# First loads in another order, tables through Pool's queue, and D0's probabilities in a zero-padded field of 384 queries

## The chip, the cores and the metric

One core of a Trainium2 chip runs the whole program. The metric is the device time of one execution in microseconds; the kernel before takes 1674.26 us (median of three runs, 1674.24 to 1674.72). Engines: TensorE (PE; its weight loads are PEld), VectorE (DVE), ScalarE (ACT), GpSimd (POOL) and SyncE (SP), which here only issues DMAs. DMAs issued by SP go through queue q1, those issued by Pool through q0.

## The reference

Two layers of an encoder on 512 tokens of 1024 features. In each layer the normed input is projected to queries, keys and values of four attention branches, to gates and to merge weights. A is a banded attention (128 either way) with 8 query heads on 2 key heads, a learned bias by distance and a sink; B a difference of two dense attentions with bias; C a dense one with rotated queries and keys; D three groups of 8 heads with strides 1, 4 and 16, each in a band of 64 either way (in its own stride) with bias, joined by their softmax sums.

```python
for l in range(DEPTH):
    h = _rmsnorm(x, norm_gain[l])
    p = _project(h, w_in[l])
    ...  # oa, ob, oc, od from p; biases from rel_bias by bucketed distance
    for n, o in enumerate((oa, ob, oc, od)):
        gated = o * jax.nn.silu(p['gate'][..., n * BRANCH_W:(n + 1) * BRANCH_W])
        y = gated @ w_branch[l, n]
        merged = merged + jax.nn.sigmoid(p['merge'][..., n * D_MODEL:(n + 1) * D_MODEL]) * y
    x = x + merged @ w_out[l]
```

Group D0 (stride 1) is what the second half of the change is about: query i sees keys i - 64 to i + 64.

## The kernel before

**Split numbers.** Matmuls run in fp16 on pairs (high part, low part). A weight piece of 1 MB comes as two fp32 halves (`wst`, `dma_w`, L118), which `load_w` (L129) splits: ScalarE makes `whi` (L142), VectorE `wlo` (L143). Activations lie transposed in `hT_h` and `hT_l`. One projection is three matmuls per 128 features (L396 to L398 for token-major results, L407 to L409 for feature-major ones), so a token tile of 512 columns takes 24.

**Start.** SP loads x tile 0, the norm gain, weight piece 0, x tile 1, piece 1, x tile 2, a small table `rb`, the one-hot table `oh` (97 rows of 4,864 bytes), x tile 3, and then weights. `wst` has three buffers, so the fourth half waits until VectorE is done with the first. `norm_a` (L209) norms a token tile; `norm_b` (L229) transposes it on TensorE into PSUM (L253) and splits it from there; `norm_t` (L239) splits first and transposes by DMA. Tiles 0 to 2 take `norm_b`, tile 3 takes `norm_t`.

**Bias lines.** The biases depend on distance alone. `bias_lines` (L260) multiplies `oh` by the table of 36 heads' biases (L274), six products with results on 8 partitions (one a head), copied into `acc`. One DMA (L929) then writes `lines` in DRAM: 23 copies of 8 rows of 2,432 numbers (9,728 bytes), 1.79 MB. `load_bias` (L536) reads a bias tile from the copies, so that each partition gets its shift. In the code the products stand behind the first token tile of the A queries, the write behind A's keys and values.

**Small tables.** Pool loads gain tables, the rotation table and the setup tables (`gain_tables`, `setup_columns`, `setup`) through its own queue at the start of the program; VectorE works them up.

**Order.** The Tile framework orders each engine's instructions by a simulated timeline; `tc.issue_after(x)` keeps what stands under it behind instruction x. `weave` interleaves the steps of an attention with those of projections. Every engine runs in order.

**D0.** `attn_d0` (L797). For a head, scores are taken for four blocks of 128 keys (kb), each against the queries from 64 ahead of the block to 64 behind it, a field of 256 columns (192 for the first and last block). ScalarE and VectorE turn them into probabilities `ph` (high) and `pl` (low). The value products for a block of 128 queries (qb) take the probabilities as the stationary operand. From the block's own keys all 128 queries count; from the block ahead only the first 64, from the one behind only the last 64. So `lo` and `hi`, 64 partitions each, are products of their own, and the first and last query blocks have their own block cut in two as well. A head has ten products of 64 queries and two of 128, each of three matmuls (`pv_mm`, L563). A's values (L658) have ten products of 128 queries a head.

Of the kernel before, what the change touches and what calls it, by code (L numbers as in the profile page):

```python
# [85 lines left out]
)  # L86
PIECE = 128 * 2048
AHEAD = 3


@with_exitstack
def encoder(ctx, tc, x, wf, norm_gain, qk_gain, sink, lambda_vec, sub_gain, rel_bias, onehot, rope, out):
# [83 lines left out]
    def load_x(src, tt):  # L176
        if tt % 2 == 0:
            x_sb[tt // 2] = qk.tile([128, 2, D], F32, tag="qx", name="xt", bufs=2)
        nc.sync.dma_start(out=x_sb[tt // 2][:, tt % 2, :], in_=src[tt * 128:tt * 128 + 128, :])

    gain_b = {}

# [19 lines left out]
    load_x(x, 1)  # L202
    with tc.issue_after(dma_w(1).ins):
        load_x(x, 2)
        nc.sync.dma_start(out=rb, in_=bass.AP(tensor=rel_bias.tensor, offset=rel_bias.offset, ap=[[0, 3], [36, 32], [1, 36]]))
        nc.sync.dma_start(out=oh, in_=onehot)
        load_x(x, 3)

    def norm_a(l, tt):  # L209

        xt = x_sb[tt // 2][:, tt % 2, :]
        ss = sm.tile([128, 2], F32, tag="n_ss", name="ss")
        for j in range(2):
# [6 lines left out]
        S.activation(rs, ln, AF.Exp, scale=-0.5)  # L220
        hs = []
        for j in range(2):
            f = slice(512 * j, 512 * j + 512)
            h = tmp.tile([128, 512], F32, tag="gs", name="h", bufs=4)
            V.scalar_tensor_tensor(h, xt[:, f], rs, gain_b[l][:, f], op0=ALUm, op1=ALUm)
            hs.append(h)
        return hs

    def norm_b(tt, hs):  # L229

        for j in range(2):
            tr = transpose4(hs[j])
            d = slice(4 * j, 4 * j + 4)
            c = slice(tt * 128, tt * 128 + 128)
            S.activation(hT_h[:, d, c], tr, AF.Copy, scale=SH)
            done = V.scalar_tensor_tensor(hT_l[:, d, c], tr, SH, hT_h[:, d, c], op0=ALUm, op1=ALUs)
        return done

    def norm_t(tt, hs):  # L239

        hi = tmp.tile([128, 2, 512], F16, tag="st", name="h_hi", bufs=3)
        lo = tmp.tile([128, 2, 512], F16, tag="st", name="h_lo", bufs=3)
# [17 lines left out]
    def bias_lines():  # L260

        V.tensor_scalar(rb, rb, SB, None, op0=ALUm)
        V.tensor_copy(rb16[0:96, :], rb)
        for a in (32, 64):
            r = slice(a, a + 32)
            V.tensor_tensor(rb[r, :], rb[r, :], rb16[r, :], op=ALUs)
            V.tensor_copy(rb16[r, :], rb[r, :])
        V.tensor_tensor(rb16[64:96, :], rb[64:96, :], rb16[64:96, :], op=ALUs)
        for i, (s0, ln_, h0, nh, off, w) in enumerate(SEG.values()):
            for e in range(0, ln_, 512):  # L270
                n = min(512, (ln_ + 1 - e))
                c = slice(s0 + e, s0 + e + n)
                p = ps_mm.tile([128, 512], F32, tag="mm", name="p")
                PE.matmul(p[:8, :n], rb16[:, h0:h0 + 8], oh[:, c], start=True, stop=True)  # L274
                if i % 2:
                    S.activation(accf[0:8, c], p[:8, :n], AF.Copy, scale=1.0 / SB)
                else:
                    V.tensor_scalar(accf[0:8, c], p[:8, :n], 1.0 / SB, None, op0=ALUm)
# [165 lines left out]
    def proj_q(res, l, kind, col, perm=False):  # L444
# [4 lines left out]
        for tt in range(NT):  # L449
# [9 lines left out]
            st = tmp.tile([128, 4, 4, HD], F16, tag="st", name="st", bufs=3)  # L459
# [10 lines left out]
    def proj_k(res, l, kind, col, perm=False):  # L470
# [6 lines left out]
        for tt in range(NT):  # L477
# [4 lines left out]
            st = tmp.tile([128, 16, 128], F16, tag="st", name="st", bufs=3)  # L482
            hi = st[:, 0:8, 0:HD]
            S.activation(hi, heads(kg), AF.Copy, scale=KS)
            V.scalar_tensor_tensor(st[:, 8:16, 0:HD], heads(kg), KS, hi, op0=ALUm, op1=ALUs)
            V.tensor_copy(st[:, :, HD:128], st[:, :, 0:HD])
            nc.sync.dma_start_transpose(out=kk[:, :, tt * 128:tt * 128 + 128], in_=st.rearrange("p a d -> p (a d)"))
            yield

    VS = SV / PROJ  # L490
# [20 lines left out]
    def proj_kv(res, l, kind, col):  # L511
# [6 lines left out]
        for tt in range(NT):  # L518
# [7 lines left out]
            st = tmp.tile([128, 4, 128], F16, tag="st", name="st", bufs=3)  # L526
# [59 lines left out]
    def gated(n, ft, gd):  # L586

        if ft == 0:
            gT[n] = big.tile([128, 4, 2, T], F16, tag="gT", name="gT", bufs=2)
        st = tmp.tile([128, 2, 512], F16, tag="st", name="st", bufs=3)  # L590
# [206 lines left out]
    def attn_d0(l, qs, kk, rsk, v):  # L797
        bias, o, n12 = {}, {}, {}

        def scores(h):  # L800
            if h % 4 == 0:
                bias[h // 4] = load_bias("D0", h, 4, "bias_d0")
            ph, pl = new_p()
            for kb in range(4):
                q0, q1 = max(128 * kb - 64, 0), min(128 * kb + 192, T)
                n, f0 = q1 - q0, q0 - (128 * kb - 64)
# [2 lines left out]
                s_mm(p, kk[:, h, ks], kk[:, 8 + h, ks], qs[:, h, q0:q1])  # L809
                t = at.tile([128, 512], F32, tag="t", name="t", bufs=3)[:, :n]  # L810
                V.scalar_tensor_tensor(t, p, rsk[:, kb, h:h + 1], bias[h // 4][:, h % 4, f0:f0 + n], op0=ALUm, op1=ALUa)  # L811
                f = slice(f0, f0 + n)
                probs(t, n, nm[:, l, 12 + h:13 + h], ph[:, kb, f], pl[:, kb, f])
            return ph, pl

        def values(h, pp):
# [6 lines left out]
                                  in_=dsc[2][hp].rearrange("(t p) e -> p t e", p=128))  # L823
            pv = ps_pv.tile([128, 4, 66], F32, tag="pv", name="pv")
            for qb in range(4):
                vt = [v[:, k, h] for k in range(4)]
                lo, hi = pv[0:64, qb, 0:65], pv[64:128, qb, 0:65]
                if qb > 0:
                    k = qb - 1
                    pv_mm(lo, ph[:, k, 192:256], pl[:, k, 192:256], vt[k], HD, True, False)  # L830
                if qb < 3:
                    k = qb + 1
                    pv_mm(hi, ph[:, k, 0:64], pl[:, k, 0:64], vt[k], HD, True, False)
                if qb == 0:
                    pv_mm(lo, ph[:, 0, 64:128], pl[:, 0, 64:128], vt[0], HD, True, True)
                    pv_mm(hi, ph[:, 0, 128:192], pl[:, 0, 128:192], vt[0], HD, False, True)
                elif qb == 3:
                    pv_mm(lo, ph[:, 3, 64:128], pl[:, 3, 64:128], vt[3], HD, False, True)
                    pv_mm(hi, ph[:, 3, 128:192], pl[:, 3, 128:192], vt[3], HD, True, True)
                else:  # L840
                    pv_mm(pv[:, qb, 0:65], ph[:, qb, 64:192], pl[:, qb, 64:192], vt[qb], HD, False, True)
# [73 lines left out]
    for l in range(L):  # L915
# [5 lines left out]
        if l:  # L921
            norm_t(3, last)
        else:
            bias_lines()
            with tc.issue_after(normed.ins):
                gain_tables(0)
        run(qa, proj_kv(r, l, "A", 512))
        if l == 0:
            nc.sync.dma_start(out=lines.rearrange("c h n -> h c n"),  # L929
                              in_=accf[0:8, 0:LINE].unsqueeze(1).to_broadcast([8, COPIES, LINE]))  # L930
            with tc.issue_after(normed.ins):
                setup_columns()
                setup()
        weave(attn_a(l, r["qA"], *r["kA"], r["vA"]),
# [90 lines left out]
```

## Time and profile before

| | |
|---|---|
| median of the runs | 1674.26 us |
| the profiled execution | 1674.46 us |
| its span (first to last instruction) | 1672.4 us |
| TensorE busy | 1602.6 us (96%) |
| VectorE busy | 1075.9 us (64%) |
| ScalarE busy | 961.0 us (57%) |
| Pool busy | 8.8 us (1%) |
| mean granted TensorE clock | 0.985 |

Busy time is the union of an engine's instructions. TensorE's matmuls overlap in the pipeline, so its pace is read from their starts. In the slices a digit is the busy share of a fortieth of the span in tenths; PEclk is the clock granted to TensorE, where 0.5 stands for its level of 1.2 GHz and 1.0 for 2.4. In a timeline row stand start, duration, engine, line and operation, out<-in, count, and in brackets the idle time ahead and what ended it.

### The profile page before, as it was taken

How to read it: one execution, taken by the hardware profiler on the slowest of the kernel's cores; microseconds unless marked ns; L12 is line 12 of the kernel's file. 1: busy time of each engine (PE TensorE's matmuls, PEld its weight loads, DVE VectorE, ACT ScalarE, POOL GpSimd, SP SyncE). 2: the span in 40 equal slices, each digit the busy share in tenths (PEclk: the TensorE clock that was granted, in tenths of full speed). 3: DMA queues.
4: the chain of work that ended last, by engine and by line, in shares of the span. 5: the costliest groups of instructions: out<-in, count | busy, mean ns of one | idle time of the engine just before them, and what ended most of it. 6: DMA issues, size and time to landing. Idle time of an engine off the chain costs nothing.

```text
span 1672.4 us, 26438 instructions
## 1 busy us (share of the span) xinstructions
PE 1602.6 (96%) x10302; PEld 834.6 (50%) x10302; DVE 1075.9 (64%) x2104; ACT 961.0 (57%) x1771; POOL 8.8 (1%) x32
## 2 busy tenths in 40 slices
PE   3389999999999999999999999999999999999999
PEld 1155545564555554454445554556455555445444
DVE  3368866785576766575556887678457676657451
ACT  3157676566664656564545767556667464556450
POOL 1000000000000000000000000000000000000000
PEclk8699999999999999999999999999999999999999
DMA  5974733352356757435357483336235674753421
GB/s 188 97 161 133 164 109 95 100 133 76 110 121 155 183 144 191 141 114 143 109 169 173 105 183 119 93 101 133 76 98 130 152 180 132 200 146 94 133 88 51
DMA packets 230817, 218.37 MB, mean 131 GB/s; under 512 B 176316, under 2 KB 188620, under 8 KB 230509
## 3 DMA queue, kind: packets, MB, share of 16 engines
q1 hardware_dynamic: 229925, 214.26, 50.0%
q0 software_dynamic: 768, 2.43, 0.5%
q8 instruction: 80, 1.31, 0.3%
q14 instruction: 44, 0.36, 0.1%
HBM read 163.94 MB, written 10.24 MB: 104 GB/s over the span
## 4 chain that ended last, share of the span: by engine, by line
PE 89%; DMA 6%; DVE 3%; ACT 1%; issue 0%; SPq 0%; DVEq 0%; ACTq 0%
PE mm L396 15%; PE mm L397 15%; PE mm L398 15%; PE mm L407 10%; PE mm L409 10%; PE mm L408 10%; PE s L560 3%; PE s L561 3%; PE pv L565 3%; DMA hT_h<-h_hi 2%; PE pv L567 2%; PE pv L566 2%; DMA oh<-in_onehot_dram 1%; DMA wst<-in_wf_dram 1%; DMA qs<-st 1%; DVE wlo L143 1%
## 5 line engine op out<-in xcount | busy, mean ns | idle before, releaser
L396 PE MATMUL mm<-whi,hT_h 128*128 128x512 f16 (+1 forms) x1408 | 522.7, 371 | 38.7 <-DMA hT_h<-h_hi 31.1
L397 PE MATMUL mm<-wlo,hT_h 128*128 128x512 f16 (+1 forms) x1408 | 522.6, 371 | 0.7 <-DVE wlo L143 0.7
L398 PE MATMUL mm<-whi,hT_l 128*128 128x512 f16 (+1 forms) x1408 | 522.2, 371 | 1.2 <-DMA hT_l<-h_lo 1.2
L143 DVE SCALAR_TENSOR_TENSOR wlo<-wst,whi 128x1024 f16<-128x1024 f32 (+1 forms) x260 | 307.3, 1204 | 203.1 <-ACT whi L142 202.0
L142 ACT ACTIVATE whi<-wst 128x1024 f16<-128x1024 f32 (+1 forms) x260 | 262.6, 1036 | 269.4 <-PE mm L408 122.3
L396 PEld LDWEIGHTS <-hT_h 128*128 128x128 f16 x1408 | 144.4, 103 | 175.9 <-DMA hT_h<-h_hi 32.1
L398 PEld LDWEIGHTS <-hT_l 128*128 128x128 f16 x1408 | 144.4, 103 | 147.6 <-issue 2.6
L397 PEld LDWEIGHTS <-hT_h 128*128 128x128 f16 x1408 | 144.4, 103 | 146.4 <-issue 7.7
L407 PE MATMUL mm<-hT_h,whi 128*128 128x512 f16 x512 | 194.1, 379 | 0.0
L409 PE MATMUL mm<-hT_h,wlo 128*128 128x512 f16 x512 | 194.1, 379 | 0.0
L408 PE MATMUL mm<-hT_l,whi 128*128 128x512 f16 x512 | 194.0, 379 | 0.0
L551 ACT ACTIVATE t<-t,nm 128x512 f32<-128x512 f32 (+2 forms) x224 | 132.0, 599 | 69.1 <-DVE t L811 24.1
L556 DVE TENSOR_TENSOR pl<-t,ph 128x512 f16<-128x512 f32 (+2 forms) x224 | 119.1, 543 | 37.8 <-ACT ph L555 36.5
L565 PE MATMUL pv<-v,ph 128*128 128x65 f16 (+2 forms) x992 | 123.8, 202 | 0.1
L566 PE MATMUL pv<-v,ph 128*128 128x64 f16 (+2 forms) x992 | 122.9, 201 | 0.0
L567 PE MATMUL pv<-v,pl 128*128 128x65 f16 (+2 forms) x992 | 121.0, 199 | 0.0
L409 PEld LDWEIGHTS <-wlo 128*128 128x128 f16 x768 | 75.1, 98 | 88.9
L407 PEld LDWEIGHTS <-whi 128*128 128x128 f16 x768 | 75.1, 98 | 87.1
L408 PEld LDWEIGHTS <-whi 128*128 128x128 f16 x768 | 75.1, 98 | 86.6
L555 ACT ACTIVATE ph<-t 128x512 f16<-128x512 f32 (+2 forms) x224 | 110.9, 506 | 2.8 <-PE pv L567 0.7
L560 PE MATMUL s<-qs,kk 128*128 128x512 f16 (+4 forms) x384 | 99.4, 293 | 1.7 <-DVE gs L582 1.3
L561 PE MATMUL s<-qs,kk 128*128 128x512 f16 (+4 forms) x384 | 100.5, 292 | 0.0
(173 smaller groups left out, 1925.4 us busy)
## 6 DMA issues: line engine op xcount, KB each, us to landing
wst<-in_wf_dram SPq DMA_DIRECT2D x264, 512.0 KB
dsc<-num SPq DMA_DIRECT2D x16, 260.0 KB
xt<-in_x_dram SPq DMA_DIRECT2D x8, 512.0 KB
bias_b<-lines SPq DMA_DIRECT2D x8, 448.0 KB
bias_a<-lines SPq DMA_DIRECT2D x16, 192.0 KB
num<-dsc SPq DMA_DIRECT2D x8, 260.0 KB
n<-dsc SPq DMA_DIRECT2D x8, 260.0 KB
bias_d<-lines SPq DMA_DIRECT2D x32, 64.0 KB
```

Of the source, the lines that this page charges most:

```text
L142: S.activation(hi[:, a], st[:, e:e + step], AF.Copy if sc is SW else AF.Identity, scale=sc)
L143: V.scalar_tensor_tensor(lo[:, a], st[:, e:e + step], sc, hi[:, a], op0=ALUm, op1=ALUs)
L396: PE.matmul(p[:, :ncol], a, wh, start=(k == 0), stop=False)
L397: PE.matmul(p[:, :ncol], a, wl, start=False, stop=False)
L398: PE.matmul(p[:, :ncol], b, wh, start=False, stop=(k == 7))
L407: PE.matmul(p, wh[:, k, f], rh[:, k], start=(k == 0), stop=False)
L408: PE.matmul(p, wh[:, k, f], rl[:, k], start=False, stop=False)
L409: PE.matmul(p, wl[:, k, f], rh[:, k], start=False, stop=(k == nk - 1))
L561: PE.matmul(p, klo, q, start=False, stop=True)
L565: PE.matmul(o, ph, vt[:, 0:d + 1], start=start, stop=False)
L566: PE.matmul(o[:, 0:d], ph, vt[:, d + 2:2 * d + 2], start=False, stop=False)
L567: PE.matmul(o, pl, vt[:, 0:d + 1], start=False, stop=stop)
```

## The change

SP loads x, gain and the first two weight pieces, and then only weights. `wst` has five buffers. `rb` and `oh` go to Pool's queue, where all tables stand behind a copy of one element of the last x tile (`there`). All four token tiles of the first layer go through `norm_b`. The products of the bias lines stand behind A's keys and values. Their stationary operand `rbr` now holds 16 copies of a segment's 8 heads (five copies on VectorE), so results lie on 128 partitions, and two DMAs on Pool's queue write `lines` from 128 and from 56 partitions. Keys (16 blocks of 128) are split and transposed in two halves. In D0 the field is 384 columns wide, the outer 64 on both sides set to zero by Pool, and each value product takes 128 columns.

```diff
+WST = 5
-            st = wp.tile([128, 1024], F32, tag="wst", name="wst", bufs=3)
+            st = wp.tile([128, 1024], F32, tag="wst", name="wst", bufs=WST)
...
         load_x(x, 2)
-        nc.sync.dma_start(out=rb, in_=bass.AP(tensor=rel_bias.tensor, offset=rel_bias.offset, ap=[[0, 3], [36, 32], [1, 36]]))
-        nc.sync.dma_start(out=oh, in_=onehot)
-        load_x(x, 3)
+        last_x = load_x(x, 3)
+
+    there = const.tile([128, 1], F32, name="there")
+    tables = G.tensor_copy(there, x_sb[1][:, 1, 0:1])
...
+        rbr = const.tile([97, len(SEG), 128], F16, name="rbr")
         for i, (s0, ln_, h0, nh, off, w) in enumerate(SEG.values()):
+            V.tensor_copy(rbr[:, i].rearrange("p (c h) -> p c h", h=8),
+                          rb16[:, h0:h0 + 8].unsqueeze(1).to_broadcast([97, 16, 8]))
...
-                PE.matmul(p[:8, :n], rb16[:, h0:h0 + 8], oh[:, c], start=True, stop=True)
+                PE.matmul(p[:, :n], rbr[:, i], oh[:, c], start=True, stop=True)
...
+        for c0, c1_ in ((0, 16), (16, COPIES)):
+            nc.gpsimd.dma_start(out=lines[c0:c1_].rearrange("c h n -> (c h) n"), in_=accf[0:8 * (c1_ - c0), 0:LINE])
 
     for tt in range(NT):
-        normed = (norm_b if tt < 3 else norm_t)(tt, norm_a(0, tt))
-        if tt < 2:
-            load_w(tt)
+        normed, split = norm_b(tt, norm_a(0, tt))
+        if tt == 0:
+            with tc.issue_after(scaled[0].ins):
+                load_w(0)
+            with tc.issue_after(split.ins):
+                load_w(1)
...
+            for pp in (ph, pl):
+                G.memset(pp[:, :, 0:64], 0.0)
+                G.memset(pp[:, :, 320:384], 0.0)
...
-                f = slice(f0, f0 + n)
+                f = slice(f0 + 64, f0 + 64 + n)
...
-                vt = [v[:, k, h] for k in range(4)]
-                lo, hi = pv[0:64, qb, 0:65], pv[64:128, qb, 0:65]
...
+                kbs = [k for k in (qb - 1, qb, qb + 1) if 0 <= k < 4]
+                for kb in kbs:
+                    f = slice((qb - kb + 1) * 128, (qb - kb + 2) * 128)
+                    pv_mm(pv[:, qb, 0:65], ph[:, kb, f], pl[:, kb, f], v[:, kb, h], HD, kb == kbs[0], kb == kbs[-1])
...
-            bias_lines()
-            with tc.issue_after(normed.ins):
+            with tc.issue_after(normed.ins), tc.issue_after(tables.ins):
                 gain_tables(0)
+                nc.gpsimd.dma_start(out=rb, in_=bass.AP(tensor=rel_bias.tensor, offset=rel_bias.offset,
+                                                        ap=[[0, 3], [36, 32], [1, 36]]))
+                nc.gpsimd.dma_start(out=oh, in_=onehot)
         run(qa, proj_kv(r, l, "A", 512))
         if l == 0:
-            nc.sync.dma_start(out=lines.rearrange("c h n -> h c n"),
-                              in_=accf[0:8, 0:LINE].unsqueeze(1).to_broadcast([8, COPIES, LINE]))
+            bias_lines()
```

SP's queue at the start of the program, before (`xt` are x tiles, `hT_h` the transposed activations):

```order
L179 DMA xt<-in_x_dram 128x1024
L186 DMA gain_b<-in_norm_gain_dram 128x1024
L125 DMA wst<-in_wf_dram 128x1024 x2
L179 DMA xt<-in_x_dram 128x1024
L125 DMA wst<-in_wf_dram 128x1024 x2
L179 DMA xt<-in_x_dram 128x1024
L205 DMA rb<-in_rel_bias_dram 96x1x36
L206 DMA oh<-in_onehot_dram 97x2432
L179 DMA xt<-in_x_dram 128x1024
L125 DMA wst<-in_wf_dram 128x1024 x3
L929 DMA lines<-acc 8x23x2432
```

The same queue after the change:

```order
L180 DMA xt<-in_x_dram 128x1024
L187 DMA gain_b<-in_norm_gain_dram 128x1024
L126 DMA wst<-in_wf_dram 128x1024 x2
L180 DMA xt<-in_x_dram 128x1024
L126 DMA wst<-in_wf_dram 128x1024 x2
L180 DMA xt<-in_x_dram 128x1024 x2
L126 DMA wst<-in_wf_dram 128x1024 x9
L478 DMA_TRANSPOSE qs<-st 128x8x128 x2
```

The tables and `lines` have left it, the last x tile stands ahead of all weights but the first two pieces, and nine weight halves stand ahead of the first query transposes.

TensorE behind A's keys and values, after the change (L281 the products of the bias lines, L575 and L576 the scores of A's first head, L409 to L411 gate 0):

```order
L281 MATMUL p<-oh,rbr 128x512
L575 LDWEIGHTS kk
L575 MATMUL s<-qs,kk 128x384
L576 LDWEIGHTS kk
L576 MATMUL s<-qs,kk 128x384
L281 LDWEIGHTS rbr
L281 MATMUL p<-oh,rbr 128x384
L281 LDWEIGHTS rbr
L281 MATMUL p<-oh,rbr 128x256
L281 LDWEIGHTS rbr
L281 MATMUL p<-oh,rbr 128x256
L409 LDWEIGHTS hT_h
```

Before, the same six products (L274) stood between the second and the third token tile's transposes. Now they stand between the first three scores, and 52 products of gate 0 follow ahead of the next score.

TensorE at a head of D0, before (the first of its 12 products; the shape's first number is the queries):

```order
L409 MATMUL mm<-gT,wlo 128x512
L565 LDWEIGHTS ph
L565 MATMUL pv<-v,ph 64x65
L566 LDWEIGHTS ph
L566 MATMUL pv<-v,ph 64x64
L567 LDWEIGHTS pl
L567 MATMUL pv<-v,pl 64x65
```

and after:

```order
L422 MATMUL mm<-gT,wlo 128x512
L580 LDWEIGHTS ph
L580 MATMUL pv<-v,ph 128x65
L581 LDWEIGHTS ph
L581 MATMUL pv<-v,ph 128x64
L582 LDWEIGHTS pl
L582 MATMUL pv<-v,pl 128x65
```

The heads stay where they were between the merge products; a head's 36 matmuls are 30.

## Rows read from the trace of the kernel before

**Rows 1.** The page: busy time of the engines, and two of the lines of slices.
```profile
PE 1602.6 (96%) x10302; PEld 834.6 (50%) x10302; DVE 1075.9 (64%) x2104; ACT 961.0 (57%) x1771; POOL 8.8 (1%) x32
...
PE   3389999999999999999999999999999999999999
...
PEclk8699999999999999999999999999999999999999
```

**Rows 2.** Waits of TensorE: total us, times, longest; the two largest.
```profile
PE mm L396 <- DMA hT_h<-h_hi: 31.1, 2, 30.2
PE p L274 <- DMA oh<-in_onehot_dram: 15.3, 1, 15.3
```

**Rows 3.** Windows: length, busy us (count) by engine, clock, DMA share, GB/s.
```profile
0.00:48.10 48.10, 20.04 (x65) 8.45 (x66) 20.09 (x38) 20.59 (x48) 4.67 (x18) 0.79 0.53 172
48.10:114.65 66.55, 34.41 (x196) 19.94 (x194) 30.02 (x82) 17.89 (x49) 1.07 (x2) 0.77 0.97 142
114.65:131.60 16.95, 15.69 (x78) 7.34 (x77) 10.75 (x21) 13.88 (x27) 0.00 (x0) 1.00 0.34 78
2.00:6.00 4.00, 0.00 (x0) 0.00 (x0) 0.07 (x1) 1.35 (x5) 3.30 (x8) 1.00 0.90 265
30.00:38.00 8.00, 0.00 (x0) 0.00 (x0) 0.00 (x0) 0.00 (x0) 0.00 (x0) 0.50 0.06 26
60.00:80.00 20.00, 0.00 (x0) 0.00 (x0) 0.00 (x0) 0.00 (x0) 0.00 (x0) 0.53 1.32 72
857.00:862.00 5.00, 5.00 (x25) 2.27 (x24) 3.30 (x6) 2.98 (x8) 0.00 (x0) 1.00 0.72 238
700.00:800.00 100.00, 100.00 (x724) 50.28 (x722) 63.32 (x146) 55.27 (x103) 1.25 (x3) 1.00 0.42 118
```

**Rows 4.** Timeline of the start: TensorE's first products and four rows around the stalls.
```profile
11.69 0.61 PE L396 MATMUL mm<-whi,hT_h 128*128 128x512 f16 x1 [2.05 <-ACT hT_h L235]
...
13.82 0.40 SPq L206 DMA_DIRECT2D oh<-in_onehot_dram  x1
...
38.03 1.01 PE L274 MATMUL p<-oh,rb 97*8 97x512 f16 x2 [15.27 <-DMA oh<-in_onehot_dram]
...
44.25 0.31 SPq L929 DMA_DIRECT2D lines<-acc  x1
...
56.13 25.60 SPq L247 DMA_TRANSPOSE hT_h<-h_hi  x1
```

**Rows 5.** Timeline: one token tile's norm, and the first score with its bias.
```profile
14.93 0.63 ACT L215 ACTIVATE sq<-xt 128x512 f32<-128x512 f32 x1 [1.31 <-DMA xt<-in_x_dram]
...
19.59 1.28 DVE L236 SCALAR_TENSOR_TENSOR hT_l<-tr,hT_h 128x512 f16<-128x512 f32 x2
...
114.65 1.00 DVE L653 SCALAR_TENSOR_TENSOR t<-s,rsk,bias_a 128x256 f32<-128x256 f32 x2
```

**Rows 6.** Timeline of TensorE: A's first value products, then D0's in two places.
```profile
131.38 0.38 PE L398 MATMUL mm<-whi,hT_l 128*128 128x512 f16 x1
131.60 0.19 PE L565 MATMUL pv<-v,ph 128*128 128x65 f16 x1
...
132.51 0.27 PE L560 MATMUL s<-qs,kk 128*128 128x256 f16 x1
...
704.36 0.38 PE L409 MATMUL mm<-gT,wlo 128*128 128x512 f16 x1
704.67 0.23 PE L565 MATMUL pv<-v,ph 128*64 128x65 f16 x2
...
705.99 0.26 PE L560 MATMUL s<-qs,kk 128*128 128x192 f16 x1
...
730.13 0.25 PE L561 MATMUL s<-qs,kk 128*128 128x192 f16 x1
730.30 0.22 PE L565 MATMUL pv<-v,ph 128*64 128x65 f16 x1
...
730.49 0.39 PE L407 MATMUL mm<-hT_h,whi 128*128 128x512 f16 x1
```

More of the change, by code (lines that the diff above doesn't have):

```diff
@@ L178, in load_x @@
             x_sb[tt // 2] = qk.tile([128, 2, D], F32, tag="qx", name="xt", bufs=2)
-        nc.sync.dma_start(out=x_sb[tt // 2][:, tt % 2, :], in_=src[tt * 128:tt * 128 + 128, :])
+        return nc.sync.dma_start(out=x_sb[tt // 2][:, tt % 2, :], in_=src[tt * 128:tt * 128 + 128, :])
     gain_b = {}
@@ L219, in norm_a @@
         rs = sm.tile([128, 1], F32, tag="n_rs", name="rs")
-        S.activation(rs, ln, AF.Exp, scale=-0.5)
+        scaled[0] = S.activation(rs, ln, AF.Exp, scale=-0.5)
         hs = []
@@ L234, in norm_b @@
             c = slice(tt * 128, tt * 128 + 128)
-            S.activation(hT_h[:, d, c], tr, AF.Copy, scale=SH)
+            split = S.activation(hT_h[:, d, c], tr, AF.Copy, scale=SH)
             done = V.scalar_tensor_tensor(hT_l[:, d, c], tr, SH, hT_h[:, d, c], op0=ALUm, op1=ALUs)
-        return done
+        return done, split
     def norm_t(tt, hs):
-        hi = tmp.tile([128, 2, 512], F16, tag="st", name="h_hi", bufs=3)
-        lo = tmp.tile([128, 2, 512], F16, tag="st", name="h_lo", bufs=3)
+        hi = tmp.tile([128, 2, 512], F16, tag="st", name="h_hi", bufs=4)
+        lo = tmp.tile([128, 2, 512], F16, tag="st", name="h_lo", bufs=4)
         for j in range(2):
@@ L273, in bias_lines @@
                 p = ps_mm.tile([128, 512], F32, tag="mm", name="p")
-                PE.matmul(p[:8, :n], rb16[:, h0:h0 + 8], oh[:, c], start=True, stop=True)
+                PE.matmul(p[:, :n], rbr[:, i], oh[:, c], start=True, stop=True)
                 if i % 2:
-                    S.activation(accf[0:8, c], p[:8, :n], AF.Copy, scale=1.0 / SB)
+                    S.activation(accf[:, c], p[:, :n], AF.Copy, scale=1.0 / SB)
                 else:
-                    V.tensor_scalar(accf[0:8, c], p[:8, :n], 1.0 / SB, None, op0=ALUm)
+                    V.tensor_scalar(accf[:, c], p[:, :n], 1.0 / SB, None, op0=ALUm)
+        for c0, c1_ in ((0, 16), (16, COPIES)):
+            nc.gpsimd.dma_start(out=lines[c0:c1_].rearrange("c h n -> (c h) n"), in_=accf[0:8 * (c1_ - c0), 0:LINE])
     for tt in range(NT):
-        normed = (norm_b if tt < 3 else norm_t)(tt, norm_a(0, tt))
-        if tt < 2:
-            load_w(tt)
+        normed, split = norm_b(tt, norm_a(0, tt))
[4 more added lines that the diff above has]
+                load_w(1)
     maxb = const.tile([128, 36], F32, name="maxb")
@@ L458, in proj_q @@
             V.tensor_tensor(heads(qn), heads(src), rs.unsqueeze(2).to_broadcast([128, 8, HD]), op=ALUm)
-            st = tmp.tile([128, 4, 4, HD], F16, tag="st", name="st", bufs=3)
+            st = tmp.tile([128, 4, 4, HD], F16, tag="st", name="st", bufs=4)
             qv = qn.rearrange("p (a b d) -> p a b d", a=4, b=2)
@@ L481, in proj_k @@
             V.tensor_tensor(heads(kg), heads(p), tabs[l][:, n:n + 1, :].to_broadcast([128, 8, HD]), op=ALUm)
-            st = tmp.tile([128, 16, 128], F16, tag="st", name="st", bufs=3)
-            hi = st[:, 0:8, 0:HD]
+            st = [tmp.tile([128, 8, 128], F16, tag="st", name="st", bufs=4) for _ in range(2)]
+            hi = st[0][:, :, 0:HD]
             S.activation(hi, heads(kg), AF.Copy, scale=KS)
-            V.scalar_tensor_tensor(st[:, 8:16, 0:HD], heads(kg), KS, hi, op0=ALUm, op1=ALUs)
-            V.tensor_copy(st[:, :, HD:128], st[:, :, 0:HD])
-            nc.sync.dma_start_transpose(out=kk[:, :, tt * 128:tt * 128 + 128], in_=st.rearrange("p a d -> p (a d)"))
+            V.scalar_tensor_tensor(st[1][:, :, 0:HD], heads(kg), KS, hi, op0=ALUm, op1=ALUs)
+            for i in range(2):
+                V.tensor_copy(st[i][:, :, HD:128], st[i][:, :, 0:HD])
+                nc.sync.dma_start_transpose(out=kk[:, 8 * i:8 * i + 8, tt * 128:tt * 128 + 128],
+                                            in_=st[i].rearrange("p a d -> p (a d)"))
             yield
@@ L525, in proj_kv @@
                 V.tensor_tensor(heads(kg), heads(p[:, 0:128]), tabs[l][:, 0:1, :].to_broadcast([128, 2, HD]), op=ALUm)
-            st = tmp.tile([128, 4, 128], F16, tag="st", name="st", bufs=3)
+            st = tmp.tile([128, 4, 128], F16, tag="st", name="st", bufs=4)
             hi, lo = st[:, 0:2, 0:HD], st[:, 2:4, 0:HD]
@@ L589, in gated @@
             gT[n] = big.tile([128, 4, 2, T], F16, tag="gT", name="gT", bufs=2)
-        st = tmp.tile([128, 2, 512], F16, tag="st", name="st", bufs=3)
+        st = tmp.tile([128, 2, 512], F16, tag="st", name="st", bufs=4)
         gf = gd.rearrange("p a b -> p (a b)")
@@ L923, in encoder @@
         else:
-            bias_lines()
-            with tc.issue_after(normed.ins):
+            with tc.issue_after(normed.ins), tc.issue_after(tables.ins):
                 gain_tables(0)
+                nc.gpsimd.dma_start(out=rb, in_=bass.AP(tensor=rel_bias.tensor, offset=rel_bias.offset,
+                                                        ap=[[0, 3], [36, 32], [1, 36]]))
+                nc.gpsimd.dma_start(out=oh, in_=onehot)
         run(qa, proj_kv(r, l, "A", 512))
         if l == 0:
-            nc.sync.dma_start(out=lines.rearrange("c h n -> h c n"),
-                              in_=accf[0:8, 0:LINE].unsqueeze(1).to_broadcast([8, COPIES, LINE]))
-            with tc.issue_after(normed.ins):
+            bias_lines()
+            with tc.issue_after(normed.ins), tc.issue_after(tables.ins):
                 setup_columns()
```

15 lines of the change are left out of this document (1 added, 14 removed).

## The prediction

> **What bounds the kernel now.** I read the page first. TensorE is busy for 96% of the span, but the two lines of slices show where it is not: the first two slices hold 3 tenths, the granted clock is down there and nowhere else [rows 1]. In the waits of TensorE two entries make nearly all of its idle time, one of 15.3 us for the one-hot table `oh` and one of 30.2 us for the transposed activations `hT_h` [rows 2]. The windows say what kind of time that is. From 30 to 38 us TensorE, VectorE and ScalarE do nothing, and the DMA engines carry 26 GB/s at a share of 0.06, a sixteenth: one engine is at work [rows 3]. From 60 to 80 us again nothing computes, at 72 GB/s. Granted clock: 0.50 and 0.53 in these windows, against 1.00 where TensorE is full. From 114.65 us on, where the first score of attention A gets its bias, TensorE is the bound: 15.69 of the next 16.95 us, and 100 of 100 us where D0 runs. So a gain can come from two places: the start, and fewer TensorE cycles later.
>
> The SP queue explains both stalls [rows 4]: `oh` is issued at 13.82 and read at 38.03, a transfer of 24 us; `lines` is issued at 44.25, the transposes of the last token tile stand behind it at 56.13, and that one instruction keeps the queue for 25.60 us. `lines` has 8 source partitions read 23 times (1.79 MB); its 36 us to 80 come to 50 GB/s.
>
> **The start, step by step.** I follow it to one event, the first value product of attention A, which begins at 131.60; all work ahead of it (96 products each for Q, K/V and gate 0, 16 score products) is in both programs.
>
> What goes: `oh` leaves the SP queue and is needed only after K/V; the last token tile is transposed on TensorE and no longer waits for `lines`. What is late next? Three things, in line.
>
> (a) x. The SP queue now carries nine transfers of 512 KB up to the fourth x tile (four x, gain, four weight halves; five staging buffers let them go without a wait). 4.7 MB at 265 GB/s, the rate of 2 to 6 us [rows 3], are 18 us; from 2 us on, with 2 us to land: 22. Pool's tables now wait for that tile: its one-element copy `there` stands ahead of all table loads on Pool's queue, so those begin at 22 too.
>
> (b) The norms of tiles 2 and 3. In the trace one tile took from its first square at 14.93 to its last `hT_l`, 19.59 + 1.28 = 20.87 [rows 5]: 5.9 us, weight splits between. Two of them from 22: 34.
>
> (c) VectorE. It does 20.09 us of work up to 48.1, where it has come about as far, and 30.02 from there to the first biased score [rows 3]. The second number is the same work after the change, now without the idle time: 34 + 30 = 64. Five copies for the replicated table and an allowance for waits between engines add 3: 67. TensorE has 48 products of 512 columns and 96 of 256 from 34 on, 10.4 + 10.5 us at the 0.216 of a 512-column one (131.38 to 131.60 [rows 6]), and isn't the bound.
>
> (d) The lines. Two Pool issues, then 1.79 MB from 128 and 56 partitions. The trace has no such write at that size; a full 128-partition stretch, the stores of x1 with loads between, ran at 238 GB/s [rows 3], which gives 7.5 us, and the 50 GB/s of the old one 36 us. I take the first, because what set the old rate in this trace was the narrow side (8 partitions); with 1.5 for the issues: 76. The bias loads wait for that on SP, with four weight halves and Q transposes behind them; 4 us to land: 80. TensorE now has 52 gate products ahead of the next score in its order, 52 x 0.216 = 11 us from about 67, so of these 13 us some 2 are idle, and VectorE stands for the rest.
>
> (e) From the first biased score (114.65 [rows 5]) to the value product (131.60 [rows 6]): 16.95 us before, TensorE the bound. With half of the gate products done, ScalarE's 13.88 busy us are the longest [rows 3]: 80 + 14 = 94.
>
> So 131.6 - 94 = 37.6 us are saved. Ends: if only TensorE's work counts, 82 (50 saved, first rival below); with the old rate of the lines, 94 + 28 = 122 (10 saved).
>
> **D0's value products.** Before, a head has ten products of 64 query columns and two of 128, three matmuls each; after, ten of 128. The page has no idle time there, so the pace of starts counts. From the last merge matmul before a head at 704.36 to the next score at 705.99 are 1.63 us, less the 0.216 that the merge matmul itself takes: 1.41. Attention A's head is the form after, ten full products: 131.38 to 132.51, less 0.216: 0.91 [rows 6]. Each of 16 heads saves 0.50: 8.0. Each run of narrow products also pays for its two ends. The piece at 730.30 has two products, and from the score ahead of it at 730.13 to the merge matmul behind it at 730.49 are 0.36; less 0.08 for that score (192 columns) and 0.06 for two products at A's pace, 0.22 is lost. Two heads of each layer are cut into three runs, two more than the others: 4 x 2 x 0.22 = 1.8. Together 9.8 us, all on TensorE.
>
> The 64 memsets on Pool (four a head) I cost at nothing: Pool is busy for 8.8 us in 32 instructions [rows 1], 0.28 each, and a buffer is free as soon as the head two back has its products, one step of the weave before ScalarE writes it again. If that cover went, four would stand ahead of ScalarE's first write: 1.1 a head, 18 us.
>
> Splitting K's transposes in two adds 32 issues on SP and moves the same bytes; the longest waits of TensorE [rows 2] hold none for K or for weights: nothing, or 1 us either way, and the same for the added staging buffers.
>
> **Sum.** 1672.4 - 37.6 - 9.8 = 1625.0 of span; the profiled execution had 1674.46 for 1672.4, so 2.1 more: 1627.1. The median shown, 1674.26, is that same time within 0.2.
>
> **Rivals.**
>
> *The start gets to TensorE's own bound.* If VectorE's work spreads better than in (c), the value product comes when TensorE's work is done: 20.04 + 34.41 + 15.69 = 70 us [rows 3] from the first product at 11.69 [rows 4]: 82. 12 less: 1615. For it: much of that 70 is at the low clock. Against: VectorE is in order and 50 of its us are needed.
>
> *The one-hot table keeps one engine on Pool's queue as well.* Row: 97 partitions went at 26 GB/s, one engine [rows 3]. If Pool's queue does it so, `oh`, from about 24, lands at 42 to 48; the loads of sub-gain, bias maximum, sink and lambda stand behind it, and VectorE stops at the sub-gain scale, which is due some 5 us after (b), at 39, with the Q splits and two weight pieces behind it, for which K/V waits. 4 to 10 us: 1634. The Trainium skill, "DMA: Bandwidth & Descriptors", section "Why a DMA increments its semaphore by 16 and not by 1", has this as a rule: a DMA takes as many engines as the largest number up to 16 that divides both slowest dimensions, so 1 for 97 rows. The trace agrees (the share of 0.06). The page also names an exception, software queues that spread odd counts over most engines; by the rule this rival holds, by the exception the forecast. No run here shows which.
>
> *D0 gains nothing*: the memsets hold ScalarE back, or the wide products cost what two narrow ones did, since narrow pairs overlap in the trace (the row at 704.67 holds two). 1627 + 10 = 1637.
>
> *The lines stay slow* at the old 50 GB/s: 1627 + 28 = 1655.
>
> *Slower than before.* The write of `lines` sits on one engine: 1.79 MB at 26 GB/s are 69 us instead of 7.5. Everything from the first biased score waits for it: 1627 + 61 = 1688. It decides from 55 us on, about 33 GB/s. Against: the trace's one-engine transfer had 97 rows, a prime, and 128 and 56 are none.
>
> **Chances.** Forecast 0.53 (1620 to 1634), TensorE's bound 0.14, one engine for `oh` 0.15, no gain in D0 0.08, slow lines 0.06, one engine for the lines 0.03, the rest 0.01. The range reaches over half of the first rival and over the second and third: 1612 to 1642, and leaves out 0.18. No change means within 0.2% (3 us), about what can be told here; only the last rival or a sum of all misfortunes comes near: faster 0.96, same 0.01, slower 0.03.
>
> **What would show it.** The waits of TensorE lose the entries for `oh` and `hT_h` of the first layer. The first value product stands at 90 to 98. VectorE is over 80% busy between 34 and 67. The `lines` packets are done within 10 us of their issue. A D0 head spans 1.13 us from merge matmul to score. It is wrong if a window without any compute of over 8 us is left after 25 us, or if 128-column heads take over 1.4 us.

## The result, and the profile of the changed kernel

The changed kernel takes 1625.39 us, the median of four runs (1623.15 to 1629.19), against 1674.25 of the kernel before on the same chip: a ratio of 0.971, 95% interval 0.9691 to 0.9729, or 48.9 us. The forecast was 1627.0, faster. The profiled execution had 1624.7, 1622.9 of it span.

The page's busy lines, TensorE's slices and the clock, which answer to [rows 1]:

```profile
PE 1593.1 (98%) x10214; PEld 834.1 (51%) x10214; DVE 1074.9 (66%) x2141; ACT 956.9 (59%) x1771; POOL 28.9 (2%) x101
...
PE   7899999999999999999989999999999999999999
...
PEclk9999999999999999999999999999999999999999
```

The first slices are filled, and one 8 is new in the middle. TensorE's waits say which is which (total us, times, longest; answering to [rows 2]):

```profile
PE tr L257 <- DVE h L229: 8.7, 2, 7.8
PE mm L411 <- DMA hT_l<-h_lo: 6.0, 1, 6.0
PE mm L409 <- DVE qn L471: 4.7, 3, 2.2
PE s L575 <- DVE t L668: 2.1, 1, 2.1
PE s L575 <- DMA kk<-st: 1.9, 2, 1.4
```

The 30.2 us for `hT_h` and the 15.3 for `oh` are gone. The 6.0 us for `hT_l` are new: before, the waits at that place were 1.2 and 1.0 us. It isn't in the start but between the two layers.

Windows of the changed kernel (length; PE, PEld, DVE, ACT, POOL busy; clock; DMA share; GB/s), answering to [rows 3]:

```profile
2.00:6.00 4.00, 0.00 (x0) 0.00 (x0) 0.16 (x1) 1.45 (x6) 0.00 (x0) 1.00 0.91 294
6.00:16.00 10.00, 7.92 (x27) 3.67 (x27) 8.01 (x14) 8.04 (x21) 0.00 (x0) 1.00 1.00 400
...
0.00:16.00 16.00, 7.92 (x27) 3.67 (x27) 8.17 (x15) 10.75 (x26) 1.12 (x12) 1.00 0.87 325
16.00:34.00 18.00, 14.31 (x67) 7.51 (x66) 16.50 (x30) 12.44 (x30) 6.42 (x10) 0.83 1.06 346
34.00:61.00 27.00, 22.45 (x148) 14.29 (x146) 25.23 (x80) 15.20 (x42) 0.53 (x1) 0.94 0.74 166
61.00:74.17 13.17, 11.64 (x52) 5.09 (x51) 0.33 (x3) 1.95 (x3) 1.07 (x2) 0.96 0.71 212
74.17:87.51 13.34, 12.66 (x54) 5.67 (x54) 9.95 (x20) 11.89 (x24) 0.00 (x0) 0.87 0.20 64
```

Pool's one-element copy shows when the last x tile was there:

```profile
16.08 1.07 POOL L209 COPY there<-xt 128x1 f32<-128x1 f32 x1 [14.26 <-DMA xt<-in_x_dram]
```

From 34 to 61 VectorE is 93% busy and by that share sets the pace (no run tests it); from 61 to 74 it does next to nothing (0.33 us), and the chain of waits names why (start, us, what):

```profile
61.74 0.53 POOL lines L288
62.28 7.93 DMA lines<-acc
...
70.36 3.78 DMA bias_a<-lines
74.17 1.02 DVE t L668 x2
```

TensorE's timeline at attention A's first value product, which answers to 131.60 of [rows 6], and a D0 head:

```profile
87.51 0.19 PE L580 MATMUL pv<-v,ph 128*128 128x65 f16 x1
...
668.01 0.38 PE L422 MATMUL mm<-gT,wlo 128*128 128x512 f16 x1
668.23 0.19 PE L580 MATMUL pv<-v,ph 128*128 128x65 f16 x1
...
669.14 0.24 PE L575 MATMUL s<-qs,kk 128*128 128x192 f16 x1
```

**Where the 49.5 us of span come from.** The same instruction can be found in both traces, and the distance of its two starts is the lead so far. It is 44.1 at the first value product (131.60 - 87.51). Across D0 of layer 0 these rows of VectorE stand ahead and behind; first the kernel before:

```profile
683.15 0.69 DVE L496 SCALAR_TENSOR_TENSOR v<-mm,v 128x512 f16<-128x512 f32 x1 [4.49 <-ACT v L495]
...
808.06 0.69 DVE L868 TENSOR_TENSOR acc<-acc,sig 128x512 f32<-128x512 f32 x1
```

and the changed one:

```profile
637.35 0.69 DVE L511 SCALAR_TENSOR_TENSOR v<-mm,v 128x512 f16<-128x512 f32 x1 [4.49 <-ACT v L510]
...
757.10 0.69 DVE L874 TENSOR_TENSOR acc<-acc,sig 128x512 f32<-128x512 f32 x1
```

683.15 - 637.35 = 45.8 and 808.06 - 757.10 = 51.0: D0 gives 5.2. Between the layers the lead falls to 44.4, and D0 of layer 1 brings it to 49.8. So: start 44.1, 1.7 around 350 us, where a wait of 1.6 for `v` of the kernel before did not come, D0 5.2 + 5.4, the layer boundary -6.6; 49.8, of which 49.5 are left at the end.

**The new stall.** SP's queue between the layers, before:

```profile
875.28 2.01 SPq L247 DMA_TRANSPOSE hT_h<-h_hi  x1
877.39 0.77 SPq L125 DMA_DIRECT2D wst<-in_wf_dram  x1
878.26 2.20 SPq L247 DMA_TRANSPOSE hT_l<-h_lo  x1
880.56 0.52 SPq L125 DMA_DIRECT2D wst<-in_wf_dram  x1
881.17 1.25 SPq L542 DMA_DIRECT2D bias_a<-lines  x2
```

and after:

```profile
824.30 1.81 SPq L251 DMA_TRANSPOSE hT_h<-h_hi  x1
826.21 1.27 SPq L126 DMA_DIRECT2D wst<-in_wf_dram  x2
827.58 1.82 SPq L251 DMA_TRANSPOSE hT_l<-h_lo  x1
829.49 1.41 SPq L557 DMA_DIRECT2D bias_a<-lines  x2
```

One weight half has moved from behind token tile 2's second transpose to ahead of it, and the bias loads now follow that transpose directly. A DMA reports that its data are in by sixteen receipts, and whoever waits needs all of them. Eight of this transpose's came at 834.9 to 835.0, the other eight at 837.8, when the second bias load was done. TensorE's row behind the wait:

```profile
837.84 0.61 PE L411 MATMUL mm<-whi,hT_l 128*128 128x512 f16 x1 [6.03 <-DMA hT_l<-h_lo]
```

and the two windows from there on:

```profile
837.80:843.70 5.90, 5.86 (x14) 2.04 (x15) 0.76 (x2) 0.72 (x2) 0.00 (x0) 0.51 0.73 153
843.70:848.00 4.30, 4.30 (x29) 2.70 (x28) 1.12 (x2) 1.10 (x3) 0.00 (x0) 1.00 0.00 0
```

The wait costs 6.0 instead of 1.2 + 1.0; after it the granted clock is at the lower level (0.51) for 13 products, 0.43 instead of 0.216 each, 2.8 more: 3.8 + 2.8 = 6.6.

### The profile page after: what moved, and what is told of

Its sections match the earlier page's. It is cut to its first block, busy times and chain, and to the rows that moved or that the text cites. A ratio compares the mean times of both kernels' runs of the same rounds, so it can differ in the third digit from the quotient of the medians.

```text
span 1622.9 us, 26502 instructions
## 1 busy us (share of the span) xinstructions
PE 1593.1 (98%) x10214; PEld 834.1 (51%) x10214; DVE 1074.9 (66%) x2141; ACT 956.9 (59%) x1771; POOL 28.9 (2%) x101
## 4 chain that ended last, share of the span: by engine, by line
PE 94%; DMA 2%; DVE 1%; issue 0%; ACT 0%; POOL 0%; SPq 0%
PE mm L411 17%; PE mm L409 17%; PE mm L410 17%; PE mm L421 10%; PE mm L420 10%; PE mm L422 10%; PE s L575 3%; PE s L576 3%; PE pv L581 2%; PE pv L582 2%; PE pv L580 2%; DMA hT_l<-h_lo 1%; DMA lines<-acc 0%; DVE wlo L144 0%; DMA gb<-in_qk_gain_dram 0%
## 5 line engine op out<-in xcount | busy, mean ns | idle before, releaser
L411 PE MATMUL mm<-whi,hT_l 128*128 128x512 f16 (+1 forms) x1408 | 523.0, 372 | 6.0 <-DMA hT_l<-h_lo 6.0
L409 PE MATMUL mm<-whi,hT_h 128*128 128x512 f16 (+1 forms) x1408 | 523.4, 372 | 4.9 <-DVE qn L471 4.7
L143 ACT ACTIVATE whi<-wst 128x1024 f16<-128x1024 f32 (+1 forms) x260 | 256.8, 1034 | 145.5 <-PE mm L421 121.5
L411 PEld LDWEIGHTS <-hT_l 128*128 128x128 f16 x1408 | 144.4, 103 | 153.0 <-DMA hT_l<-h_lo 6.5
L409 PEld LDWEIGHTS <-hT_h 128*128 128x128 f16 x1408 | 144.4, 103 | 143.4 <-issue 4.2
L581 PE MATMUL pv<-v,ph 128*128 128x64 f16 (+1 forms) x960 | 118.3, 201 | 0.0
L580 PE MATMUL pv<-v,ph 128*128 128x65 f16 (+1 forms) x960 | 118.2, 200 | 0.0
L582 PE MATMUL pv<-v,pl 128*128 128x65 f16 (+1 forms) x960 | 116.5, 199 | 0.0
L429 ACT ACTIVATE sq<-mm 128x512 f32<-128x512 f32 (+1 forms) x96 | 51.8, 539 | 90.0 <-PE mm L411 88.8
L575 PE MATMUL s<-qs,kk 128*128 128x512 f16 (+4 forms) x384 | 99.8, 293 | 4.1 <-DVE t L668 2.1
```

The lines of the kernel that those rows point to most:

```text
L143: S.activation(hi[:, a], st[:, e:e + step], AF.Copy if sc is SW else AF.Identity, scale=sc)
L409: PE.matmul(p[:, :ncol], a, wh, start=(k == 0), stop=False)
L411: PE.matmul(p[:, :ncol], b, wh, start=False, stop=(k == 7))
L575: PE.matmul(p, khi, q, start=True, stop=False)
L580: PE.matmul(o, ph, vt[:, 0:d + 1], start=start, stop=False)
L581: PE.matmul(o[:, 0:d], ph, vt[:, d + 2:2 * d + 2], start=False, stop=False)
```

## The experiments

The theory after the result: the start is worth 44 us and hangs on the load rate, on VectorE and then on the lines' write; D0 gives 10.6; the fifth staging buffer costs 6.6 between the layers.

**1. D0 alone.** The kernel before with the changed `attn_d0`, nothing else:

```diff
+            for pp in (ph, pl):
+                G.memset(pp[:, :, 0:64], 0.0)
+                G.memset(pp[:, :, 320:384], 0.0)
...
+                    pv_mm(pv[:, qb, 0:65], ph[:, kb, f], pl[:, kb, f], v[:, kb, h], HD, kb == kbs[0], kb == kbs[-1])
```

> The kernel before with D0's padded field and wide value matmuls alone; start and staging as before. Aligning the two traces instruction by instruction, VectorE's lead over the kernel before grows by 5.2 us across layer 0's D0 (45.80 to 50.96) and by 5.4 across layer 1's (44.37 to 49.77). Theory (the wide heads save about 0.65 us each, and the 6 us that TensorE waits for hT_l between the layers belongs to the other edits): 1674.25 - 10.5 = 1663.7 us, and a wait between the layers as before, 0.9 and 1.2 us. Rival (the wait between the layers comes from D0's new timing): 1670 us with a wait of about 6 us there. Rival (the lead inside D0 comes from something in the start): no change, 1674.

Measured 1664.99 us, ratio 0.9941 (0.9926 to 0.9956), 9.8 less than the 1674.81 of the kernel before measured with it. The wait for `hT_l` is 1.8 us. So D0 gains by itself, and the new stall isn't its doing.

**2. Three staging buffers.**

```diff
-WST = 5
+WST = 3
```

> The changed kernel with three weight staging buffers instead of five. Theory (the fourth and fifth buffer let one more weight half stand on SP's queue ahead of the transpose of token tile 2 between the layers, and its last receipts fall behind the bias loads): the 6.0 us wait for hT_l shrinks to about 1, the fall of the clock behind it goes, 6.6 us saved there; in the start the fourth weight half now waits for the first split (from 8.3 us), so the last x tile lands 0 to 3 us later than 16.1: together 1619 to 1622 us. Rival (the wait between the layers comes from the four smaller st buffers or the K transposes cut in two, which stay): the wait stays at 6 us, 1625 to 1628.

Measured 1623.77 us, 0.9694 (0.968 to 0.9709). Waits of TensorE between the layers:

```profile
PE mm L411 <- DMA hT_l<-h_lo: 1.5, 1, 1.5
PE mm L409 <- DMA hT_h<-h_hi: 1.1, 1, 1.1
PE mm L409 <- DVE v L511: 1.0, 1, 1.0
```

The stall is back to what it was, and the lead over the changed kernel grows by 6.1 us there; the smaller `st` buffers and the halved K transposes, which stay, are cleared. But the start lost 4.1 to 4.6 us where I allowed 3: SP took 7.80 us to issue the second weight piece, most of it waiting for a buffer, and the last x tile reached Pool's copy at 17.99 instead of 16.08. The lines' write also took 10.65 us in this trace, where the changed kernel's has 7.93, so not all of the loss belongs to the buffers. The median is 1.6 below the changed kernel's, not the 3 to 6 I expected, and the two intervals overlap: that the stall is gone is read from the traces, not from the time.

**3 and 10. The order between the layers, mended twice.** In run 3 the weight loads are queued behind tile 2's transposes, and the bias loads behind tile 3's, which are traced ahead of Q:

```diff
+            with tc.issue_after(held[0]) if held[0] is not None else nullcontext():
+                dma = nc.sync.dma_start(out=st, in_=src[:, e:e + 1024])
...
+            with tc.issue_after(held[0]) if held[0] is not None and j == 0 and kind == "A" and h0 == 0 else nullcontext():
+                nc.sync.dma_start(out=t[:, j, :],
...
-        next(qa)
         if l:
+            held[0] = moved[0].ins
             norm_t(3, last)
+        next(qa)
```

> The changed kernel with the issue order between the layers mended: the weight loads of layer 1's first pieces are queued behind the transposes of token tile 2, the last tile's transposes are traced ahead of Q, and the first bias_a loads are queued behind them; the start is the same. Theory (the 6.0 us wait for hT_l is a matter of the order on SP's queue): waits between the layers below 1.5 us in sum, 1625.4 - 6.6 = 1619 us. Rival (the bytes are the bound there, so the wait moves to the weights of K/V, to the bias or to the last tile's transposes): 1623 to 1626.

Measured 1620.53 us, 0.9676 (0.9662 to 0.9691). The one wait left there is `PE mm L413 <- DVE qn L475`, 2.2 us, where under 1.5 was expected; the lead grows by 5.7 across the boundary. In run 10 only the bias loads are held:

> The changed kernel with one edit between the layers: layer 1's first bias_a loads are queued behind the last tile's transposes; the weight halves stay ahead of the transpose of token tile 2. In the changed kernel half of that transpose's receipts came at 834.9 to 835.0, the other half at 837.8, when the bias loads behind it were done. Theory (the wait of 6.0 us has two parts, about 2 from the one weight half more ahead and 2.8 from the bias loads behind): the wait shrinks to about 3.2 us, 1625.4 - (2.8 to 4) = 1621 to 1623. Rival (all of it is the weight half, and the late receipts are those of slow engines in any case): the wait stays at 6 us, 1625.

Measured 1620.92 us, 0.9687 (0.9674 to 0.97). TensorE's wait:

```profile
832.95 0.39 PE L414 MATMUL mm<-whi,hT_l 128*128 128x512 f16 x1 [2.54 <-DMA hT_l<-h_lo]
```

2.5 instead of 6.0: the larger part of the wait was the bias loads, issued *behind* the transpose. Its sixteen receipts now come together, at 832.76 to 832.90. After this shorter wait the clock falls too (0.66 from 833 to 838). Holding the loads gains 3.8 us there, the rest of the 4.5 lies in the start's scatter (below).

**4. The lines from 8 partitions**, in the new place and on Pool's queue:

```diff
-        for c0, c1_ in ((0, 16), (16, COPIES)):
-            nc.gpsimd.dma_start(out=lines[c0:c1_].rearrange("c h n -> (c h) n"), in_=accf[0:8 * (c1_ - c0), 0:LINE])
+        nc.gpsimd.dma_start(out=lines.rearrange("c h n -> h c n"),
+                            in_=accf[0:8, 0:LINE].unsqueeze(1).to_broadcast([8, COPIES, LINE]))
```

> The changed kernel with lines written the old way, from 8 partitions read 23 times in one DMA, but in the new place and on Pool's queue. Theory (the narrow side sets the rate, 50 GB/s before against 1.79 MB in 7.9 us now): lines lands 28 us later, the first biased score too, 1625.4 + 28 = 1653 us. Rival (the old rate came from SP's queue and its place behind other transfers; Pool's queue gives it the full rate): 1625 to 1628. Rival (fewer, wider descriptors on one engine): over 1680.

Measured 1654.17 us, 0.9872 (0.9855 to 0.9888), 28.8 more than the changed kernel. The chain of waits:

```profile
62.43 41.61 DMA lines<-acc
104.09 3.77 DMA bias_a<-lines
```

1.79 MB in 41.6 us are 43 GB/s on the other queue: the narrow side set the old rate, not SP's queue. What in the narrow side does it, the eight partitions or the engines that serve them, no run separates.

**5. Pool's tables at once.**

```diff
-    there = const.tile([128, 1], F32, name="there")
-    tables = G.tensor_copy(there, x_sb[1][:, 1, 0:1])
```

> The changed kernel without the one-element copy that holds Pool's tables behind the last x tile: Pool's loads go out from about 1.5 us, as before the change, beside the x and weight loads on SP. Theory (the rate I took, 265 GB/s, was that of SP's loads shared with Pool's tables; alone they run at 325 over the first 16 us): about 1.2 MB more go ahead of or beside x, the last x tile lands at 19 to 21 instead of 16.1, the first value product moves from 87.5 by 0 to 3 us: 1625 to 1629 us. Rival (the rate is that of the first microseconds of any load, and the tables take nothing from x): the last tile still at 16, the tables are there early, 1622 to 1625.

Measured 1627.38 us, 0.9722 (0.9708 to 0.9737). Its windows:

```profile
2.00:6.00 4.00, 0.00 (x0) 0.00 (x0) 0.16 (x1) 1.36 (x5) 3.96 (x9) 1.00 0.87 270
6.00:16.00 10.00, 6.46 (x19) 2.93 (x20) 5.20 (x8) 3.77 (x8) 0.69 (x2) 1.00 1.03 308
```

All bytes together make 270 and 308 GB/s, where x and weights alone made 294 and 400; the last tile's last receipt comes at 22.68 instead of 16.02, and it is squared from 23.44 instead of 17.82. So the tables do take from x. The first biased score then comes at 78.78, 4.6 later. The first value product is only 0.4 later (87.92), but from 150 us to D0 the run trails the changed kernel by 2 to 3 us, and 2 us between the medians are within the runs' scatter: the wait for the tile is worth 0 to 3 us.

**6. The one-hot table on SP's queue**, right behind the last x tile:

```diff
+        nc.sync.dma_start(out=oh, in_=onehot)
...
-                nc.gpsimd.dma_start(out=oh, in_=onehot)
```

> The changed kernel with the one-hot table loaded on SP's queue right behind the last x tile, as one DMA of 97 rows, instead of Pool's queue. Theory (97 rows on SP's queue use one engine of 16, on Pool's queue most of them; 460 KB at 26 GB/s are 18 us against about 3): oh lands at 34 to 40, still ahead of its first use at 55, but the weight halves issued behind it cannot land before it on that engine: 1626 to 1636 us, a stretch with a DMA share near a sixteenth. Rival (the queue makes no difference): oh in some 3 us, 1624 to 1627.

Measured 1643.37 us, 0.982 (0.9805 to 0.9834), 18.0 more than the changed kernel and above the range expected. A window:

```profile
32.00:36.00 4.00, 0.00 (x0) 0.00 (x0) 0.00 (x0) 0.00 (x0) 0.00 (x0) 0.50 0.07 27
```

and ScalarE's next weight split:

```profile
40.06 1.06 ACT L143 ACTIVATE whi<-wst 128x1024 f16<-128x1024 f32 x1 [19.75 <-DMA wst<-in_wf_dram]
```

One engine of 16, with the table's last packet ending at 38.3 us, and the weight halves issued behind it wait. On SP's queue no more than two of the 97 packets are in flight at once; on Pool's queue, in the changed kernel, they all lie between 22.3 and 26.7 us, with up to 17 at once, so on at least nine engines if two an engine is the most there as well. The Trainium skill, "DMA: Bandwidth & Descriptors", section "Why a DMA increments its semaphore by 16 and not by 1", is borne out in both halves: one engine for 97 rows on a hardware queue, most engines on a software queue.

**7. Four times the zero fills** in D0 (`for pp in (ph, pl, ph, pl, ph, pl, ph, pl)`).

> The changed kernel with each of D0's zero fills on Pool done four times, 16 a head instead of 4. Theory (hidden: Pool has about 0.3 us of each, 5 us a head against heads some 9 us apart): no change, 1623 to 1628 us. Rival (no slack: ScalarE's first write into the field already waits for the last fill): 12 x 0.3 more in each of 16 heads, 1640 to 1680.

Measured 1626.15 us, 0.9715 (0.9696 to 0.9733). The traced run lags the changed kernel by 4.8 us ahead of layer 0's D0 and by 4.8 behind it (the lag is from the start, where the lines' write took 10.9 us): the fills are hidden, with room for four times as many.

**8, 9 and 11. The lines' write off the path**, all on top of run 3. Run 8 calls `bias_lines()` ahead of the K/V projection:

> The version with the held loads between the layers, and the bias lines made and written ahead of the K/V projection instead of behind it. In the changed kernel VectorE stands for 12.84 us until bias_a has come from lines, and TensorE lives on gate products meanwhile. Theory (the lines' write of about 8 us then lies beside VectorE's K/V work, so the first biased score comes when VectorE is free, from 74 to 64 to 68, and the first value product goes to TensorE's own bound of about 82): 1620.5 - (2 to 6) = 1615 to 1618 us. Rival (the first bias loads now stand ahead of Q's transposes on SP's queue and hold them while lines is written): 1621 to 1627.

Measured 1622.97 us, 0.9699 (0.9683 to 0.9715): a miss. The lines left at 41.90 instead of 61.74, but TensorE, in order, now stood 7.3 us for the table's own operand (`PE p L285 <- DVE rbr L279`). Run 9 writes A's 512 columns into a tile of their own, first, and A's bias loads read from that:

```diff
+            if i == 0:
+                write(lines_a, 0, 512)
...
+        write(lines[:, :, 512:], 512, LINE)
```

> The version with the held loads between the layers, and attention A's share of the bias lines (512 of 2432 columns) written into a DRAM tile of its own as soon as its copy is done, ahead of the other segments. In the changed kernel the first biased score comes at 74.17, behind 7.93 us of lines and 3.78 us of bias_a, while VectorE stands for 12.84 us; in other runs the same write took 10.8. Theory (the start's end hangs on that write alone): 0.38 MB take 2 to 4 us from an issue at about 57, bias_a lands at 63 to 66, the first value product at TensorE's own bound of about 82 instead of 87.5 to 89: 1620.5 - (4 to 7) = 1614 to 1617 us. Rival (the bias loads now wait on SP's queue ahead of the last K transpose, and ScalarE's exponentials are the next to be late): 1618 to 1622.

Measured 1621.35 us (1616.69 to 1623.77), 0.9678 (0.9665 to 0.9691): a miss too. The first biased score came at 64.80, 9.4 earlier, but the chain of waits shows what was next:

```profile
63.31 9.88 DMA kk<-st
...
73.24 0.39 PE s L587
```

K's last transpose took 9.9 us beside the write of the other columns, and the first value product came at 92.77. This trace is of the slowest of the five runs; the fastest was as fast as run 11. In run 11 that write waits for the transpose:

```diff
+            after_k = G.tensor_copy(k_there, r["kA"][0][:, 3, T - 1:T])
+            with tc.issue_after(after_k.ins):
+                write(lines[:, :, 512:], 512, LINE)
```

> As the version with attention A's share of the lines written first, but the other 1920 columns are held on Pool's queue behind a one-element copy of the last K tile, so their write doesn't run beside K's last transpose. There the transpose was issued at 63.31 and the score that reads it began at 73.24, with lines packets of up to 5 us in between. Theory (that write was what held K's last tile): the transpose lands within 3 us, the waits for kk fall from 9.4 to under 4 us in sum, the first value product comes at 82 to 86 instead of 92.8, 1614 to 1617 us. Rival (the bias loads ahead of the transpose on SP's queue hold it by themselves): the waits for kk stay above 6 us, 1618 to 1622.

Measured 1616.7 us (1616.45 to 1618.56), 0.9663 (0.965 to 0.9676), first value product at 85.11:

```profile
PE s L585 <- DMA kk<-st: 4.9, 3, 2.5
```

The time and the product lie in the ranges expected. But K's last transpose still took 5.4 us, not under 3, and the waits for `kk` are 4.9, not under 4: the write of the other columns was a part of the 9.9, not all of it. The intervals of runs 9 and 11 overlap, so what holding the write is worth in time is not shown. Run 11 is the fastest version here.

**12. Run 3 again**, on the chip of run 11.

> The version with the held loads between the layers once more, on the same chip as the one above: 1620.5 us if the first measurement holds (1619.9 to 1621.6 there); the two differ by more than 2 us if the split of the lines pays, by less if it doesn't.

Measured 1621.27 us (1620.52 to 1624.41), 0.9691 (0.9676 to 0.9705). The runs of 11 and 12 don't overlap; 4.6 us lie between the medians.

## Why the prediction was right, and where only its sum was

The time came out 1.6 us from the forecast, by two errors of opposite sign. That it came so close is luck. The sources of the gain are the ones the prediction named, and runs 1, 4 and 6 show three of them one by one: the wide heads, the wide lines, and `oh` off SP's queue.

- **(a), the load of x, was mis-sized.** I took 265 GB/s from 2 to 6 us [rows 3] and got 22; the tile was in Pool's hands at 16.08. Those four microseconds were shared with Pool's tables, which the change itself moves away, and the rate of later microseconds is higher: 400 GB/s from 6 to 16, 308 with the tables back. In run 5, with them back, the tile's last receipt comes at 22.68, close to the 22.
- **(b) and (c).** The last norm ended at 33.1 (forecast 34) although x was 6 earlier: VectorE had taken in weight splits meanwhile, 24.7 us of work by 34 (8.17 + 16.50) where 20.09 were counted. That was work counted in (c), so the last copy for the lines came at 61.2 instead of 67. By 61 VectorE had done 49.9 us of work, the 50.1 that (c) adds up. VectorE as the bound fits its 93% from 34 to 61.
- **(d)** held in size: the lines in 7.9 us where 7.5 stood, bias at 74.17 where 80 stood, 9 + 4 us after the copies in both. TensorE's stall there was 2.1 (forecast 2). Run 4 shows the price of the old form, 28.8 by the medians against 28; in its trace the write took 41.6 us instead of 36, and the run ends 32.2 behind.
- **(e)**: 13.3 us for 14. The start saved 44.1 for 37.6. Of these 6.5 more, 5.8 are there at the last copy for the lines, but that (a) makes them all is not shown. Run 5 has x as late as forecast (and the tables early): its bias comes at 78.78, near the 80 of the forecast, and its first value product at 87.92, not 94, so (e) took 9.1 us there and has no fixed price. By run 5, x alone is worth 0.4 us at the first value product and up to 3 later on. Which term holds the rest stays open.
- **D0**: 10.6 in the traces and 9.8 alone (run 1), for 9.8. The head spans 669.14 - 668.01 = 1.13, the figure forecast. The fills are free (run 7). Another 1.7 us, around 350, stand in no term.
- **The step that failed** is "nothing, or 1 us either way, and the same for the added staging buffers". I looked only at whether TensorE waits for weights. A buffer more lets a load out earlier, and that load stands on SP's queue in front of something else. The new stall and the lower clock behind it cost 6.6 us; run 2 isolates the buffers (6.1 come back), runs 3 and 10 the order (5.7 and 3.8). That is as much as the start gave beyond its forecast.
- **Rivals.** One engine for `oh`: refuted on Pool's queue, true on SP's (run 6). Slow lines (7.9 us), one engine for the lines (the same) and no gain in D0 (run 1): refuted. TensorE's own bound at 82: not reached; even run 11 comes to 85.1.
- **Readings and signs.** The two waits named make 45.5 us of the 69.8 that TensorE was idle before, two thirds and not "nearly all". The first value product, at 87.51, lies ahead of the 90 to 98 given as a sign, and VectorE is 77% busy from 34 to 67, not over 80, because its work ends at 61; both follow from the start being faster than forecast. The other signs came true.

## What to carry to other kernels

More staging buffers are a change of the queue's order: look at every place where the loads that they release overtake a transfer that somebody waits for, and at what follows that transfer. For a rate, take a window in which the same queues run as will run afterwards. When a sum comes out right, align the two traces and check the terms; here +6.5 in the start and -6.6 between the layers had hidden each other.

## What the runs showed of the hardware

- A transfer can be held by one issued behind it: eight of the sixteen receipts of a 256 KB transpose came 2.8 us after the others, with the bias loads. A bias load's own data gave eight receipts. When only those loads were moved (run 10), the sixteen came within 0.2 us and the wait fell from 6.0 to 2.5 us.
- The lines' write of 1.79 MB took 7.5 to 7.9 us in some executions and 9.8 to 10.9 in others of the same form, from the same place; with it goes the start: three traces with the slow write and the changed kernel's start (runs 3, 7 and 12) lag its trace by 1.4 to 4.8 us ahead of the layer boundary. That it makes part of the 6 us among the changed kernel's runs is likely, not shown, and what decides it was not found.
- A transpose of K beside such a write took 9.9 us (run 9), with lines packets of up to 5 us in the same microseconds; with the write held it took 5.4 (run 11), and others of its kind 2.5 to 3.9.
